# Post-norm gains reduced inside the merge, block sums of h formed ahead of attention, and four more chunks as block products

## The chip, the cores and the metric

The kernel runs on one core of a Trainium2 chip. The metric is device time in microseconds, as the median of runs of the whole kernel; a profiled execution gives the trace. Engines are called by their names in the profile: PE is TensorE (matmuls; PEld its weight loads), DVE is VectorE, ACT is ScalarE, POOL is GpSimd, SP is the engine whose queue issues nearly all transfers.

## The reference

One layer of a backbone works on x (512 tokens x 1024) with 256 context tokens, all in fp32:

```python
sh, sc, gt = _modulation(c, w_mod, b_mod)          # silu(c) @ w_mod + b_mod, three parts of 1024
h = _rmsnorm(x, pre_g) * (1.0 + sc) + sh           # hc likewise, from ctx and c_ctx
parts = _split_in(h @ w_in)                        # 10 parts of 1024 columns
b_gate, c_gate, x_in, z_a, q, k, v, z_b, g_a, g_b = parts
attn = _neighbourhood_attention(rope(q), rope(k), v, k_c, v_c, rpb)   # 16 heads of 64
y_a = (silu(z_a) * b_gate * _dwconv3(c_gate * x_in, conv_w, conv_b)) @ w_out_conv
y_b = (silu(z_b) * attn) @ w_out_attn
merged = sigmoid(g_a) * y_a + sigmoid(g_b) * y_b
x = x + gt * _rmsnorm(merged @ w_o, post_g)
```

The part `gt` of the modulation, times `post_g`, scales each channel of the normed output. The kernel calls these products the gains.

## The kernel before, in words

**Precision.** Every fp32 operand of a large product is held as two terms, H (a cast of the value on ACT, L67) and L (the value less H, on DVE, L70). A product is three matmuls: H·H, H·L, L·H. The helper is `split`.

**Chunks.** Weights come as chunks of 256 columns x 1024 rows, two raw tiles of 512 KB each (L89), three raw buffers per half. A chunk is used in one of two ways. Directly, it is split (two 1024-column casts and subtractions) and gives two units of 128 columns: each is 8 x 3 matmuls with 512 tokens moving (L164 to L166). Or it becomes a *pair* (`pair`, L294, with `product`, L286): the 2 x 2 blocks of weights and of h (256 tokens x 512 rows) are multiplied in seven block products in place of eight, 12 matmuls of 256 columns for each, 84 in all (L289). For that the weights' sums T1 to T4 are formed on DVE (L102 to L110), seven blocks are split in two, and results are put together by copies on ACT and adds on DVE (L306 to L317). It also needs four block sums of h, named S2, S3, S4 and X1; `block_sums` forms them once for each of four slices k. `paired` decides which chunk is a pair.

**Stages.** A first stage computes the modulation from slabs of w_mod (a multiply and reduce of 128 x 1024 on DVE for each, L379), normalises x, and multiplies h by a first set of conv columns while h comes into being. Then follow conv chunks for j=1 to 3 with the modulation of the context (`modulate_c`) between their units. The gains, eight more slabs and reductions (`gain`, L571), follow in the same stage. Behind it come queries, keys and values of the first heads (to about 137 us).

Attention walks 8 head pairs p=0 to 7 (to about 500 us), each in eight slots. PE would idle between a slot's scores and its softmax, so `plan` gives each p other chunks as filling: "qk" queries and keys of the next p, "v" values, "zb" the gate of attention's values, "cx" and "bz" conv chunks, "g" merge gates. The block sums stand in slots of p=0 and p=1. The last gate of attention's values, `gate2(3)`, comes behind the last slot.

The merge, j=0 to 7 (534 to 662 us), multiplies conv results `us` and attention results `as` by output chunks y0 to y7 (`in_wout`), with 24 + 24 matmuls each, between the remaining merge gates. At j=4 the scaled gains are copied to a 128 x 128 tile for each k (L977) and transposed by PE (L978) into `gpost`, which lies along the channels. From j=4 on, the last product is prepared: the blocks of w_o are loaded (L925), their sums T1 to T4 formed (L929), and splits made. The last product (L1008) is also in seven blocks; post norm, gains and the residual follow.

**What sets the order.** The first stage is scheduled by hand. For the rest a scheduler orders each engine's instructions by its own estimate; each engine then runs its list strictly in that order. The SP queue also is one list: a transfer that waits for a free buffer holds the later ones. The tiles' tags say which memory a tile shares: `h0` to `h7` hold h, `hc` its context counterpart, `u`, `a` and `s` tags have changing contents.

Of the kernel before, what the change touches and what calls it, by code (L numbers as in the profile page):

```python
# [27 lines left out]
def layer(ctx: ExitStack, tc, xp, ctxt, ctxT, cc, wmod, small, wfirst, win, wout, wo, rel, tab, out):  # L28
# [30 lines left out]
    hcs = [thc[k // 2][:, k % 2] for k in range(KT)]  # L59
    hc = [t[:, 0] for t in hcs], [t[:, 1] for t in hcs]  # L60
    usc = [dr.tile([P, S], F32, name=f"usc{j}") for j in range(KT)]
    asc = [dr.tile([P, 2, S], F32, name=f"asc{g}") for g in range(2)]

    def split(H, L, src, scale=None, pinned=False):

        if scale is None:
            cast = nc.scalar.copy(H, src)  # L67
            if pinned:
                tc.keep_in_program_order(cast)
            nc.vector.tensor_sub(L, src, H.bitcast(F32))  # L70
# [160 lines left out]
        "cx": lambda j: win[2 * j], "bz": lambda j: win[2 * j + 1],  # L231
    }
    def paired(n, i):
        return n == "g" or n == "qk" and i in (3, 4, 6) or n == "zb" and i < 3 or n in ("cx", "bz") and i > 4

    order = [(win[i], False) for i in range(8)] + [(qk(0), False), (vz(0, 0), False)]
    order += [(where[n](i), n if paired(n, i) else False) for f in plan for n, i in f] + [(vz(3, 1), paired("zb", 3))]
# [109 lines left out]
    def unit(w, i, m=hx):  # L347
        ps = pj()
        proj_T(ps, w, i, m)
        return ps  # L350


    with ExitStack() as p0:
# [78 lines left out]
        with tc.manual_schedule(engines={E.PE, E.DVE, E.Activation, E.SP}):  # L432
# [74 lines left out]
            for k in range(KT):  # L507
# [51 lines left out]
        def modulate_c(k):  # L559
            if k < 5:  # L560
                load_slab(k)
            condition(k, 1)
            nc.scalar.mul(cols[k, 1][:, 0:1], cols[k, 1][:, 0:1], sp[:, PG + k:PG + k + 1])
            modulate(k, 1, ctT[k], hc[0][k], hc[1][k])

        def gain(k):

            t = st.tile([P, D], F32, name="wm", bufs=6)
            nc.sync.dma_start(t, wmod[16 + k])
            junk = st.tile([P, D], F32, name="junk")  # L570
            nc.vector.tensor_tensor_reduce(  # L571
                out=junk, in0=t, in1=cb[:, 0], scale=1.0, scalar=sp[:, BM + 16 + k:BM + 17 + k],
                op0=ALU.mult, op1=ALU.add, accum_out=gains[:, k:k + 1],
            )

        ks = [5, 6, 7, 0, 1, 2, 3, 4]
        work = [lambda k=k: modulate_c(k) for k in ks] + [lambda k=k: gain(k) for k in range(KT)]
        for j in range(2, 4):
            for _ in conv(j):
                for f in work[:2]:  # L580
                    f()
                del work[:2]
        for f in work:
            f()
        nc.vector.tensor_mul(gains, gains, sp[:, QG:QG + KT])


    def block_sums():

        h0, h1 = slice(0, 256), slice(256, S)  # L590
        for n in ("S2", "S3", "S4", "X1"):
            blocks_h[n] = [], []
        for k in range(4):
            a, b = (cv.tile([P, S], F32, name="tc", bufs=3) for _ in range(2))
            for x, i in ((a, k), (b, 4 + k)):
                nc.vector.tensor_add(x, hx[0][i].bitcast(F32), hx[1][i].bitcast(F32))
            nc.vector.tensor_sub(b[:, h1], b[:, h1], a[:, h1])
            nc.vector.tensor_sub(a[:, h1], a[:, h0], a[:, h1])
            for o, x, y in ((a[:, h0], b[:, h1], a[:, h0]), (b[:, h0], a[:, h0], b[:, h0])):
                nc.vector.scalar_tensor_tensor(out=o, in0=x, scalar=-1.0, in1=y, op0=ALU.mult, op1=ALU.subtract)  # L600
            yield
            for x, names, tag in ((a, ("S2", "S3"), f"u{k}"), (b, ("S4", "X1"), ("a2", "a3", "s0", "s1")[k])):
                t = hp.tile([P, 2, S], F32R, name=f"{names[0]}{k}", tag=tag)
                split(t[:, 0], t[:, 1], x)
                for n, ts in zip(names, (h0, h1)):
                    for y in range(2):
                        blocks_h[n][y].append(t[:, y, ts])
            yield
# [218 lines left out]

    for g in (keys_queries(0), values(0)):
        for _ in g:
            pass  # L830
    later.pop()[0]()
    convs = {j: conv_pairs(j) if paired("cx", j) else conv(j) for j in range(4, KT)}
    fill = []
# [115 lines left out]
    for j in range(KT):  # L949
        w = chunk()  # L950
        g = [G[j][:, i] for i in range(2)]
        if j in (4, 6):
            raws[j // 2] = G[j]
        m2 = raws[j // 2][:, j % 2]
        for i in range(2):
            nc.vector.scalar_tensor_tensor(
                out=g[i], in0=g[i], scalar=1.0, in1=unit(w, i, ua[i]), op0=ALU.add, op1=ALU.mult
            )
            if j == 7 and i == 0:
                A2 = [bp.tile([P, 2, S], F32R, name=f"A2{k}", tag=f"us{k}") for k in range(4)]  # L960
                for k in range(3):
                    split(A2[k][:, 0], A2[k][:, 1], raws[2 + k // 2][:, k % 2])
        nc.vector.tensor_add(m2, g[0], g[1])
        if j < 4:
            for _ in merge_gates(j + 4):
                pass
        if j == 4:

            nc.vector.tensor_scalar(out=gains[:, 0:4], in0=gains[:, 0:4], scalar1=0.5, scalar2=None, op0=ALU.mult)
            nc.vector.tensor_scalar(out=gains[:, 4:8], in0=gains[:, 4:8], scalar1=-0.5, scalar2=None, op0=ALU.mult)  # L970
            gpost = bp.tile([P, D], F32, name="gpost")
            for i in range(2):
                gb = cv.tile([P, S], F32, name="ta")
                ps = pj()
                for k in range(4):
                    n = 4 * i + k
                    nc.vector.tensor_copy(gb[:, k * P:(k + 1) * P], gains[:, n:n + 1].broadcast_to([P, P]))  # L977
                    nc.tensor.transpose(ps[:, k * P:(k + 1) * P], gb[:, k * P:(k + 1) * P], ident)  # L978
                nc.scalar.copy(gpost[:, i * S:(i + 1) * S], ps)
        if j == 4:  # L980
            A11, S3 = operand("A11", hp, ("u2", "u3")), operand("S3", hp, ("a2", "a3"))
            for q in range(2):
                split(A11[q][:, 0], A11[q][:, 1], raws[q][:, :, h0])
                x = cv.tile([P, S], F32, name="tb").rearrange("p (k c) -> p k c", k=2)
                nc.vector.tensor_sub(x, raws[q][:, :, h0], raws[q][:, :, h1])
                split(S3[q][:, 0], S3[q][:, 1], x)
            B11, B12 = quarter("B11", hp, ("s0", "s1")), quarter("B12", hp, ("u0", "u1"))
            B22, B21, T2, T3 = (quarter(n, hp, (f"h{2 * i}", f"h{2 * i + 1}")) for i, n in enumerate(("B22", "B21", "T2", "T3")))
            for t, i in ((B11, (0, 0)), (B12, (0, 1)), (B22, (1, 1)), (B21, (1, 0))):
                load_block(t, *i)  # L990
# [213 lines left out]
```

## Time and profile before

| | |
|---|---|
| median of 3 runs | 708.93 us (708.57 to 709.4) |
| profiled execution | 709.01 us, span 707.2 us |
| granted clock of PE | 0.997 |
| busy PE / DVE / ACT | 695.0 / 586.3 / 436.5 us |
| matmul instructions on PE | 4196 |
| pairs among the chunks | 20 |
| moved from memory | 87.07 MB read, 5.24 MB written |

The rows of the profile name a line, an engine, an operation, the tiles written and read, and a count. The profile's page gives busy times and the chain that ended last, other views give each engine's waits, and the trace can be cut into stretches. The prediction below quotes the rows that it uses.

### The profile page before, as it was taken

How to read it: one execution, taken by the hardware profiler on the slowest of the kernel's cores; microseconds unless marked ns; L12 is line 12 of the kernel's file. 1: busy time of each engine (PE TensorE's matmuls, PEld its weight loads, DVE VectorE, ACT ScalarE, POOL GpSimd, SP SyncE). 2: the span in 40 equal slices, each digit the busy share in tenths (PEclk: the TensorE clock that was granted, in tenths of full speed). 3: DMA queues.
4: the chain of work that ended last, by engine and by line, in shares of the span. 5: the costliest groups of instructions: out<-in, count | busy, mean ns of one | idle time of the engine just before them, and what ended most of it. 6: DMA issues, size and time to landing. Idle time of an engine off the chain costs nothing.

```text
span 707.2 us, 11426 instructions
## 1 busy us (share of the span) xinstructions
PE 695.0 (98%) x4196; PEld 618.0 (87%) x4196; DVE 586.3 (83%) x1114; ACT 436.5 (62%) x868; POOL 66.9 (9%) x110
## 2 busy tenths in 40 slices
PE   7999999999999999999999999999999999999996
PEld 4888888888889989898999999999898899988885
DVE  6979997668599989978898797999799676665996
ACT  6566632656577677775876766778693444442563
POOL 0000002230130310301302203000000000000000
PEclk9999999999999999999999999999999999999998
DMA  8996896564351563542635436313733233560013
GB/s 338 406 354 227 284 339 173 131 164 144 99 105 24 135 176 116 127 138 60 168 106 165 103 125 157 101 61 105 247 117 116 87 120 120 198 250 30 31 59 120
DMA packets 37466, 108.27 MB, mean 153 GB/s; under 512 B 5025, under 2 KB 5281, under 8 KB 37410
## 3 DMA queue, kind: packets, MB, share of 16 engines
q1 hardware_dynamic: 28946, 92.20, 37.8%
q0 software_dynamic: 8320, 15.21, 10.7%
q8 instruction: 33, 0.54, 0.3%
q14 instruction: 23, 0.19, 0.1%
q10 hardware_dynamic: 144, 0.13, 0.1%
HBM read 87.07 MB, written 5.24 MB: 131 GB/s over the span
## 4 chain that ended last, share of the span: by engine, by line
PE 91%; DVE 4%; DMA 2%; ACT 1%; issue 1%; SPq 0%; POOL 0%; DVEq 0%; ACTq 0%
PE ps L289 25%; PE ps L164 11%; PE ps L166 11%; PE ps L165 11%; PE ps L177 6%; PE ps L1008 5%; PE ps L773 4%; PE ps L754 3%; PE ps L182 3%; PE ps L717 3%; PE ps L196 2%; PE ps L424 2%; PE ps L428 2%; PE ps L425 2%; DMA fraw<-in_wfirst 1%; PE ps L726 1%
## 5 line engine op out<-in xcount | busy, mean ns | idle before, releaser
L67 ACT CAST w<-raw 128x512 fp32r<-128x512 f32 (+1 forms) x193 | 137.3, 733 | 95.9 <-PE ps L166 31.3
L70 DVE TENSOR_TENSOR w<-raw,w 128x512 fp32r<-128x512 f32 (+1 forms) x193 | 156.6, 824 | 42.3 <-ACT w L67 40.9
L289 PE MATMUL ps<-S,w 128*128 128x256 f32 x960 | 121.9, 283 | 0.0
L289 PEld LDWEIGHTS ps<-S,w 128*128 128x128 f32 x960 | 118.2, 192 | 0.1
L289 PE MATMUL ps<-h,w 128*128 128x256 f32 x720 | 94.0, 284 | 0.6 <-DVE tc L306 0.5
L289 PEld LDWEIGHTS ps<-h,w 128*128 128x128 f32 x720 | 89.9, 191 | 2.5 <-DVE tc L306 0.7
L164 PE MATMUL ps<-h,w 128*128 128x512 f32 x208 | 81.5, 392 | 0.0
L166 PE MATMUL ps<-h,w 128*128 128x512 f32 x208 | 81.2, 390 | 0.0
L165 PE MATMUL ps<-h,w 128*128 128x512 f32 x208 | 81.0, 390 | 0.0
L626 POOL DMA_DIRECT2D tc<-tb x32 | 28.8, 1175 | 286.7 <-DVE tc L624 197.7
L747 ACT ACTIVATE pt<-pt,z 128x512 f32<-128x512 f32 x64 | 43.0, 724 | 6.0 <-DVE z L745 5.9
L166 PEld LDWEIGHTS ps<-h,w 128*128 128x128 f32 x208 | 39.0, 188 | 8.3
L165 PEld LDWEIGHTS ps<-h,w 128*128 128x128 f32 x208 | 39.1, 188 | 8.0
L164 PEld LDWEIGHTS ps<-h,w 128*128 128x128 f32 x208 | 39.1, 188 | 7.9
L67 ACT CAST TH<-ps 128x512 fp32r<-128x512 f32 x64 | 35.8, 589 | 15.5 <-PE ps L754 15.5
L733 DVE CUSTOM_DVE_ANT_1 ps<-ps,bt 128x512 f32<-128x512 f32 x56 | 38.8, 693 | 6.8 <-PE ps L717 6.5
L70 DVE TENSOR_TENSOR TL<-ps,TH 128x512 fp32r<-128x512 f32 x64 | 42.2, 682 | 1.0 <-ACT TH L67 0.7
L754 PE MATMUL ps<-ident,pt 128*128 128x128 f32 x256 | 33.3, 273 | 0.0
L177 PE MATMUL ps<-w,h 128*128 128x512 f32 x128 | 32.3, 394 | 0.0
L754 PEld LDWEIGHTS ps<-ident,pt 128*128 128x128 f32 x256 | 29.2, 140 | 2.1 <-ACT pt L747 0.2
L740 ACT ACTIVATE pt<-ps,m 128x512 f32<-128x512 f32 x32 | 22.0, 688 | 12.5 <-DVE m L733 11.8
L773 PE MATMUL ps<-TH,V 128*128 128x256 f32 (+1 forms) x96 | 28.5, 319 | 0.2 <-ACT TH L67 0.2
(249 smaller groups left out, 1387.8 us busy)
## 6 DMA issues: line engine op xcount, KB each, us to landing
raw<-in_win SPq DMA_DIRECT2D x74, 512.0 KB, 4.4
wm<-in_wmod SPq DMA_DIRECT2D x34, 512.0 KB, 6.4
raw<-in_wout SPq DMA_DIRECT2D x16, 512.0 KB, 3.6
bt<-in_rel SPq DMA_DIRECT2D x16, 256.0 KB, 2.9
tc<-tb POOLq DMA_DIRECT2D x32, 128.0 KB, 3.6
B<-in_wo SPq DMA_DIRECT2D x8, 512.0 KB, 6.4
fraw<-in_wfirst SPq DMA_DIRECT2D x8, 384.0 KB, 8.6
qd<-qd POOLq DMA_DIRECT2D x24, 128.0 KB, 2.3
```

The lines of the kernel that those rows point to most:

```text
L67: cast = nc.scalar.copy(H, src)
L70: nc.vector.tensor_sub(L, src, H.bitcast(F32))
L164: nc.tensor.matmul(ps, lhsT=H[k][:, cs], rhs=mH[k], start=k == 0, stop=False)
L165: nc.tensor.matmul(ps, lhsT=H[k][:, cs], rhs=mL[k], start=False, stop=False)
L166: nc.tensor.matmul(ps, lhsT=L[k][:, cs], rhs=mH[k], start=False, stop=k == KT - 1)
L177: nc.tensor.matmul(ps, lhsT=mH[k][:, ts], rhs=both[k].rearrange("p a c -> p (a c)"), start=k == 0, stop=False, skip_group_check=True,)
L289: nc.tensor.matmul(ps, lhsT=w[:, x, k], rhs=act[y][k], start=start and k + o == 0, stop=k == 3 and o == 2, skip_group_check=True,)
L733: nc.vector.tensor_tensor_reduce(out=s3, in0=s3, in1=bt[:, e::4 - e][:, 0:2], scale=-1.0, scalar=3.0e38, op0=ALU.add, op1=ALU.min, accum_o ...
L747: nc.scalar.mul(x, x, z[:, i:i + 1])
L754: nc.tensor.transpose(tp[:, c], pt[:, c * P:(c + 1) * P], ident)
L773: nc.tensor.matmul(o3[:, dst], lhsT=V[p][:, kt, h], rhs=src(t), start=n == 0 and t is TH, stop=n == len(work) - 1 and t is TL,)
L1008: nc.tensor.matmul(out, lhsT=a(x, k, ts), rhs=w[y][k // 2][:, k % 2, cols], start=start and k + o == 0, stop=k == 3 and o == 2, skip_group ...
```

## The change

It has three parts.

1. `paired` also takes in qk 2, zb 3, cx 4 and bz 4, which makes 24 pairs.
2. `block_sums` is stepped during the conv chunks j=2 and 3, once the context's modulation has been handed out, and then during the first queries, keys and values; it no longer stands in attention's slots.
3. The gains leave the conv stage. The conditioning vector after its silu is kept in a DRAM tile `csc`. In the merge, at j=4 and j=5, it is loaded again to all partitions (`cond`, in h4's memory), and the eight slabs follow through h5 to h7. Their scaling, copies and transposes move from j=4 to j=6 in the program. The blocks T2 and T3 of the last product, which use h4 to h7, come after them.

```diff
@@ layer
+    csc = dr.tile([1, D], F32, name="csc")
@@ paired
-        return n == "g" or n == "qk" and i in (3, 4, 6) or n == "zb" and i < 3 or n in ("cx", "bz") and i > 4
+        return n == "g" or n == "qk" and i in (2, 3, 4, 6) or n == "zb" or n in ("cx", "bz") and i > 3
@@ first stage
+            nc.sync.dma_start(csc, cb[0:1, 0])
             nc.sync.dma_start(cb[:, 1], cc[1:2].broadcast_to([P, D]))
@@ conv stage
-        def gain(k):
-
-            t = st.tile([P, D], F32, name="wm", bufs=6)
-            nc.sync.dma_start(t, wmod[16 + k])
-            junk = st.tile([P, D], F32, name="junk")
-            nc.vector.tensor_tensor_reduce(
...
-        ks = [5, 6, 7, 0, 1, 2, 3, 4]
-        work = [lambda k=k: modulate_c(k) for k in ks] + [lambda k=k: gain(k) for k in range(KT)]
+        ks = [5, 6, 7, 4, 0, 1, 2, 3]
+        work = [lambda k=k: modulate_c(k) for k in ks]
+        sums = block_sums()
         for j in range(2, 4):
             for _ in conv(j):
                 for f in work[:2]:
                     f()
+                if not work:
+                    next(sums)
                 del work[:2]
-        for f in work:
-            f()
-        nc.vector.tensor_mul(gains, gains, sp[:, QG:QG + KT])
@@ ahead of attention
     for g in (keys_queries(0), values(0)):
         for _ in g:
-            pass
+            next(sums, None)
@@ attention's slots
-    sums = block_sums()
...
-        if i in (4, 5, 6, 7, 12, 13, 14, 15):
-            next(sums)
@@ merge, for j in range(KT)
         if j == 4:
-
+            A11, S3 = operand("A11", hp, ("u2", "u3")), operand("S3", hp, ("a2", "a3"))
...
+            for t, i in ((B11, (0, 0)), (B12, (0, 1)), (B22, (1, 1)), (B21, (1, 0))):
+                load_block(t, *i)
+        if j in (4, 5):
+            if j == 4:
+                cond = hp.tile([P, D], F32, name="cond", tag="h4")
+                nc.sync.dma_start(cond, csc.broadcast_to([P, D]))
+            for k in range(4 * j - 16, 4 * j - 12):
+                t = hp.tile([P, D], F32, name=f"wg{k}", tag=f"h{5 + k % 3}")
+                nc.sync.dma_start(t, wmod[16 + k])
+                nc.vector.tensor_tensor_reduce(
+                    out=t, in0=t, in1=cond, scale=1.0, scalar=sp[:, BM + 16 + k:BM + 17 + k],
+                    op0=ALU.mult, op1=ALU.add, accum_out=gains[:, k:k + 1],
+                )
+        if j == 6:
+
+            nc.vector.tensor_mul(gains, gains, sp[:, QG:QG + KT])
             nc.vector.tensor_scalar(out=gains[:, 0:4], in0=gains[:, 0:4], scalar1=0.5, scalar2=None, op0=ALU.mult)
```

Three places show what the scheduler makes of it. The first is SP's queue in the merge, from the last blocks of w_o (`B`) to the input for the residual (`xr`); `raw<-in_wout` are the halves of y6 and y7. Before:

```order
L925 DMA B_7013<-in_wo 128x1024
L925 DMA B_7017<-in_wo 128x1024
L89 DMA raw<-in_wout 128x1024 x4
L1062 DMA xr_7237<-in_xp 128x1024
L1062 DMA xr_7238<-in_xp 128x1024
```

Now (`wg` are the gains' slabs):

```order
L914 DMA B_7212<-in_wo 128x1024
L970 DMA cond<-csc 128x1024
L973 DMA wg_7227<-in_wmod 128x1024
L973 DMA wg_7230<-in_wmod 128x1024
L973 DMA wg_7233<-in_wmod 128x1024
L90 DMA raw<-in_wout 128x1024
L973 DMA wg_7236<-in_wmod 128x1024
L90 DMA raw<-in_wout 128x1024
L973 DMA wg_7302<-in_wmod 128x1024
L973 DMA wg_7305<-in_wmod 128x1024
L973 DMA wg_7308<-in_wmod 128x1024
L90 DMA raw<-in_wout 128x1024
```

The load of cond and four slabs stand ahead of the second half of y6, four more slabs by y7's second half.

The second is DVE's list behind the first evictions of j=4 in the merge (`g_6233` before, `g_6453` now: one tile of gates times products). Before:

```order
L929 TENSOR_TENSOR T_7020<-B_7012,B_7014 128x1024
L956 SCALAR_TENSOR_TENSOR g_6233<-g_6233,ps 128x512
L929 TENSOR_TENSOR T_7021<-B_7013,B_7015 128x1024
L70 TENSOR_TENSOR w<-raw,w 128x4x256
L956 SCALAR_TENSOR_TENSOR g_6233<-g_6233,ps 128x512
L70 TENSOR_TENSOR w<-raw,w 128x4x256
L963 TENSOR_TENSOR g_6233<-g_6233 128x512
L956 SCALAR_TENSOR_TENSOR g_6419<-g_6419,ps 128x512
```

Now, where `L974 ISA wg` is a gain's reduction and `ISA gains` the read of its sum:

```order
L945 SCALAR_TENSOR_TENSOR g_6453<-g_6453,ps 128x512 x2
L974 ISA wg_7227,gains<-wg_7227,cond,sp 128x1024
L974 ISA gains 128x1
L952 TENSOR_TENSOR g_6453<-g_6453 128x512
L974 ISA wg_7230,gains<-wg_7230,cond,sp 128x1024
L974 ISA gains 128x1
L974 ISA wg_7233,gains<-wg_7233,cond,sp 128x1024
L974 ISA gains 128x1
L945 SCALAR_TENSOR_TENSOR g_6639<-g_6639,ps 128x512
L71 TENSOR_TENSOR w<-raw,w 128x4x256
```

The reductions stand between the evictions and the splits of y6, and the two sums into T (L929) are no longer there.

The third is PE's list around the gains' transposes (`ps<-ident,ta`). Before they stand at the end of j=4:

```order
L165 MATMUL ps<-as_6157,w 128x512
L166 MATMUL ps<-as_6157,w 128x512
L978 MATMUL ps<-ident,ta 128x128 x8
L164 MATMUL ps<-us_5956,w 128x512
L165 MATMUL ps<-us_5956,w 128x512
```

Now they stand within the first unit of j=7:

```order
L165 MATMUL ps<-us_6176,w 128x512
L166 MATMUL ps<-us_6176,w 128x512
L167 MATMUL ps<-us_6176,w 128x512
L165 MATMUL ps<-us_6179,w 128x512
L166 MATMUL ps<-us_6179,w 128x512
L990 MATMUL ps<-ident,ta 128x128
L167 MATMUL ps<-us_6179,w 128x512
L165 MATMUL ps<-us_6182,w 128x512
L166 MATMUL ps<-us_6182,w 128x512
L990 MATMUL ps<-ident,ta 128x128 x7
L167 MATMUL ps<-us_6182,w 128x512
```

One transpose comes after five matmuls of the unit, the other seven after three more.

More of the change, by code (lines that the diff above doesn't have):

```diff
@@ L350, in unit, with block_sums @@
         return ps
+    def block_sums():
+        h0, h1 = slice(0, 256), slice(256, S)
+        for n in ("S2", "S3", "S4", "X1"):
+            blocks_h[n] = [], []
+        for k in range(4):
+            a, b = (cv.tile([P, S], F32, name="tc", bufs=3) for _ in range(2))
+            for x, i in ((a, k), (b, 4 + k)):
+                nc.vector.tensor_add(x, hx[0][i].bitcast(F32), hx[1][i].bitcast(F32))
+            nc.vector.tensor_sub(b[:, h1], b[:, h1], a[:, h1])
+            nc.vector.tensor_sub(a[:, h1], a[:, h0], a[:, h1])
+            for o, x, y in ((a[:, h0], b[:, h1], a[:, h0]), (b[:, h0], a[:, h0], b[:, h0])):
+                nc.vector.scalar_tensor_tensor(out=o, in0=x, scalar=-1.0, in1=y, op0=ALU.mult, op1=ALU.subtract)
+            yield
+            for x, names, tag in ((a, ("S2", "S3"), f"u{k}"), (b, ("S4", "X1"), ("a2", "a3", "s0", "s1")[k])):
+                t = hp.tile([P, 2, S], F32R, name=f"{names[0]}{k}", tag=tag)
+                split(t[:, 0], t[:, 1], x)
+                for n, ts in zip(names, (h0, h1)):
+                    for y in range(2):
+                        blocks_h[n][y].append(t[:, y, ts])
+            yield
     with ExitStack() as p0:
@@ L564, in modulate_c @@
             modulate(k, 1, ctT[k], hc[0][k], hc[1][k])
-        def gain(k):
-            t = st.tile([P, D], F32, name="wm", bufs=6)
-            nc.sync.dma_start(t, wmod[16 + k])
-            junk = st.tile([P, D], F32, name="junk")
[L571 to L574, printed above, removed]
-        ks = [5, 6, 7, 0, 1, 2, 3, 4]
-        work = [lambda k=k: modulate_c(k) for k in ks] + [lambda k=k: gain(k) for k in range(KT)]
+        ks = [5, 6, 7, 4, 0, 1, 2, 3]
+        work = [lambda k=k: modulate_c(k) for k in ks]
+        sums = block_sums()
         for j in range(2, 4):
@@ L581, in layer @@
                     f()
+                if not work:
+                    next(sums)
                 del work[:2]
-        for f in work:
-            f()
-        nc.vector.tensor_mul(gains, gains, sp[:, QG:QG + KT])
[L588 to L608, printed above, removed]
     attn = {}
@@ L967, in layer @@
         if j == 4:
+            A11, S3 = operand("A11", hp, ("u2", "u3")), operand("S3", hp, ("a2", "a3"))
+            for q in range(2):
+                split(A11[q][:, 0], A11[q][:, 1], raws[q][:, :, h0])
+                x = cv.tile([P, S], F32, name="tb").rearrange("p (k c) -> p k c", k=2)
+                nc.vector.tensor_sub(x, raws[q][:, :, h0], raws[q][:, :, h1])
+                split(S3[q][:, 0], S3[q][:, 1], x)
+            B11, B12 = quarter("B11", hp, ("s0", "s1")), quarter("B12", hp, ("u0", "u1"))
+            B22, B21, T2, T3 = (quarter(n, hp, (f"h{2 * i}", f"h{2 * i + 1}")) for i, n in enumerate(("B22", "B21", "T2", "T3")))
+            for t, i in ((B11, (0, 0)), (B12, (0, 1)), (B22, (1, 1)), (B21, (1, 0))):
[13 more added lines that the diff above has]
+            nc.vector.tensor_mul(gains, gains, sp[:, QG:QG + KT])
             nc.vector.tensor_scalar(out=gains[:, 0:4], in0=gains[:, 0:4], scalar1=0.5, scalar2=None, op0=ALU.mult)
@@ L979, in layer @@
                 nc.scalar.copy(gpost[:, i * S:(i + 1) * S], ps)
[L980 to L990, printed above, removed]
         if j == 5:
```

## The prediction

> **What bounds the kernel now.** I read the page's busy times and the shares of its chain first, then TensorE's waits, then stretches of the trace by engine.
>
> ```profile
> PE 695.0 (98%) x4196; PEld 618.0 (87%) x4196; DVE 586.3 (83%) x1114; ACT 436.5 (62%) x868; POOL 66.9 (9%) x110
> PE 91%; DVE 4%; DMA 2%; ACT 1%; issue 1%; SPq 0%; POOL 0%; DVEq 0%; ACTq 0%
> PE ps L472 <- ACT crow L444: 3.3, 1, 3.3
> PE ps L424 <- ACT h L67: 1.2, 1, 1.2
> PE ps L289 <- DVE tc L306: 0.5, 1, 0.5
> PE ps L773 <- DVE TL L70: 0.5, 1, 0.5
> ```
>
> TensorE is 98% busy and makes 91% of the chain. It waits some 6 us in all, 4.5 of them before its first long stretch. So the time is the sum of the matmuls, and a change counts by the matmul time it removes, less the waits it creates. Behind it VectorE is busy 83%, which is little room, and unevenly spread. From here "late" means later against TensorE than before.
>
> **What a chunk gains as a pair.** A chunk of 256 output columns is either two units of 24 matmuls, each 512 columns wide, or a pair of 84 matmuls, each 256 wide. Both stand side by side in the gates and merges behind attention (chain of waits: start, length, work):
>
> ```profile
> 514.24 20.15 PE ps L289 x168
> ...
> 545.30 10.07 PE ps L289 x84
> 555.37 0.23 PE ps L164
> ...
> 566.28 10.07 PE ps L289 x84
> ```
>
> A pair takes 10.07 us (168 take 20.15: the same). Between 555.37 and 566.28 stand two units: 10.91 us for 48 matmuls, 0.227 each against 0.120. The pair saves 0.84 us. The order of the changed kernel holds 2016 matmuls of L289's kind where 1680 stood, four pairs more, so the edit is really there. **Term 1: 4 x 0.84 = 3.36 us less.**
>
> [...]
>
> **What it asks of VectorE and ScalarE.** Groups by shape (busy, mean ns | idle before):
>
> ```profile
> L70 DVE TENSOR_TENSOR w<-raw,w 128x512 fp32r<-128x512 f32 x143 | 95.7, 685 | 17.0 <-ACT w L67 15.7 <-PE ps L754 0.8
> L70 DVE TENSOR_TENSOR w<-raw,w 128x1024 fp32r<-128x1024 f32 x50 | 60.9, 1221 | 25.3 <-ACT w L67 25.2
> L102 DVE TENSOR_TENSOR raw<-raw 128x512 f32<-128x512 f32 x20 | 13.7, 685 | 0.2
> L306 DVE TENSOR_TENSOR tc<-tc,ps 128x256 f32<-128x256 f32 x12 | 4.9, 412 | 0.0
> L314 DVE SCALAR_TENSOR_TENSOR tc<-tc 128x256 f32<-128x256 f32 x12 | 5.0, 420 | 1.1 <-ACT tc L311 1.1
> L571 DVE CUSTOM_DVE_ANT_0 junk<-wm,cb,sp 128x1024 f32<-128x1024 f32 x8 | 10.3, 1282 | 0.0
> ```
>
> A pair needs 4 weight sums and 7 splits of 0.685 us and 4 evictions of about 0.415: 9.2 us. Two splits of 1.221 go. So each new pair costs VectorE 6.8 us. Block sums of one k are 4 operations of 512 columns and 4 of 256, 4.4 us; all four k, 17.6 us. The eight gains are about 10.3 us plus reads. Now the stretches that win or lose such work (busy of PE, PEld, DVE, ACT, POOL; clock; DMA share; GB/s):
>
> ```profile
> 40.00:60.00 20.00, 20.00 (x90) 16.32 (x89) 16.35 (x27) 15.10 (x25) 0.00 (x0) 1.00 0.66 235
> 138.00:182.00 44.00, 44.00 (x222) 37.23 (x221) 33.32 (x69) 27.77 (x54) 8.27 (x13) 1.00 0.47 130
> 182.00:224.00 42.00, 42.00 (x244) 36.79 (x243) 35.96 (x86) 28.63 (x68) 8.34 (x13) 1.00 0.37 87
> 486.00:545.00 59.00, 59.00 (x399) 54.51 (x399) 53.76 (x102) 41.78 (x76) 0.00 (x0) 1.00 0.44 143
> 545.00:618.00 73.00, 73.00 (x481) 67.28 (x480) 46.27 (x70) 30.64 (x51) 0.00 (x0) 1.00 0.39 131
> ```
>
> *In front of attention.* The gains' 10.3 us go, the 17.6 come. The new order starts the sums early: about 5.6 us of them fall in 40 to 60, where VectorE has 3.65 free, so the weight splits behind them come some 2 us late. Such a split is due about 3 us after it is done. I take 0 (0 to 0.8).
>
> *p=0, 138 to 182.* 10.7 us are free; two pairs add 13.6 and two k of sums leave, 8.8: 4.8 more, covered. What can still stall is a chunk that holds its raw buffers longer, so that the next chunk lands late and ScalarE queues behind its cast: 0 (0 to 0.8).
>
> *p=1, 182 to 224.* A pair adds 6.8, sums take 8.8 away: 2 us of relief, just ahead of three of TensorE's few waits, the last two on VectorE:
>
> ```profile
> 252.55 0.49 PE L773 MATMUL ps<-TH,V 128*128 128x512 f32 x1 [0.16 <-ACT TH L67]
> 253.50 0.50 PE L773 MATMUL ps<-TL,V 128*128 128x512 f32 x1 [0.45 <-DVE TL L70]
> ...
> 263.44 1.69 PE L289 MATMUL ps<-h,w 128*128 128x256 f32 x12 [0.47 <-DVE tc L306]
> ```
>
> They are 1.08 us. The work of p=2 that causes them is unchanged, and it starts behind a sync of TensorE, so I leave them: 0 (1.1 less to 0).
>
> *The last gate, 486 to 545.* 5.2 us free, 6.8 added: up to 1.5 us late until 545, behind which 26.7 are free. Successive VectorE operations overlap a little, so the true excess is nearer the low end. **Term 2: 0.2 us more (0 to 1.5).**
>
> **The gains in the merge.** SP's queue takes the load of cond and nine slabs' worth in all, 0.52 MB each; four stand ahead of output chunk y6's first load, one more ahead of its second. Before:
>
> ```profile
> 615.82 3.91 SPq L925 DMA_DIRECT2D B<-in_wo  x5
> 619.84 11.83 SPq L89 DMA_DIRECT2D raw<-in_wout  x4
> 620.00:624.00 4.00, 4.00 (x19) 3.34 (x18) 3.63 (x6) 3.97 (x6) 0.00 (x0) 1.00 0.91 306
> 624.00:628.00 4.00, 4.00 (x20) 3.30 (x19) 2.51 (x3) 0.08 (x1) 0.00 (x0) 1.00 1.01 383
> 629.01 1.05 ACT L67 CAST w<-raw 128x1024 fp32r<-128x1024 f32 x1 [4.92 <-DMA raw<-in_wout]
> 640.84 0.39 PE L164 MATMUL ps<-us,w 128*128 128x512 f32 x1
> ```
>
> The queue is full (share 1.01, 383 GB/s) until y6 lands at 629.0, and TensorE asks for y6 at 640.84. Four loads at 383 GB/s are 5.5 us: cast at 634.5, split by 636.7, 4 us in hand. The remaining slabs wait for a buffer whose reduction is done, so the eighth reduction ends at about 644 to 647. The scaled gains are copied only behind the eviction of j=6, after 651.7, so 4 us are in hand there too. Behind each reduction VectorE queues the splits of y6 and y7 and the merge's evictions. This costs 0 as long as the queue keeps its rate.
>
> *The transposes.* Eight move from the end of j=4 into j=7's first unit:
>
> ```profile
> 629.06 1.04 PE L978 MATMUL ps<-ident,ta 128*128 128x128 f32 x8
> 662.60 11.04 PE L1008 MATMUL ps<-w,A 128*128 128x512 f32 x48
> 651.72 0.39 PE L164 MATMUL ps<-us,w 128*128 128x512 f32 x1
> 626.53 1.23 DVE L929 TENSOR_TENSOR T<-B,B 128x1024 f32<-128x1024 f32 x1 [1.25 <-DMA B<-in_wo]
> 656.16 2.36 DVE L929 TENSOR_TENSOR T<-B,B 128x1024 f32<-128x1024 f32 x2
> L977 DVE COPY ta<-gains x8: 218/222/223, 538.6 to 543.2; 128x128 f32<-128x128 f32 x8
> 663.71 1.22 DVE L70 TENSOR_TENSOR w<-B,w 128x1024 fp32r<-128x1024 f32 x1
> 665.44 1.22 DVE L70 TENSOR_TENSOR w<-B,w 128x1024 fp32r<-128x1024 f32 x1
> 666.58 0.69 DVE L70 TENSOR_TENSOR A<-g,A 128x512 fp32r<-128x512 f32 x1
> ```
>
> Their own time is the same in both places. But before, the copies were long done; now each follows j=6's eviction (0.7), a scale and its copy. The first transpose stands 1.1 us into the unit, the other seven 1.9 us in, while the copies, at 0.22 each, end some 3.2 us in. TensorE waits there, and behind it the rest of that unit. **Term 3: 0.4 us more (0.2 to 1.0).**
>
> *The tail.* Two sums of the output weights, 1.2 us each, that ran by 628 (the second at 626.53), and the eight copies now stand between 652 and 665 on VectorE, together 4 us, with only a short gap to swallow them: the sums end about 3 us late. Behind them are the splits at 663.71 to 666.58. TensorE needs these from 668.05 (24 of the 48 matmuls from 662.60) to about 670, so they had 2.7 to 3.4 us in hand. **Term 4: 0.4 us more (0 to 1.0).**
>
> **Sum.** -3.36 + 0.2 + 0.4 + 0.4 = -2.36 us. The profiled execution took 709.01 (span 707.2), 0.08 over the median: 706.65 there, **706.6** as a median.
>
> **Rivals.**
> (A) *VectorE takes the bound's place.* Terms 2 to 4 at their ends (1.5, 1.0, 1.0), or p=0 for one of them: 3.4 of 3.36 eaten, about 708.9. For it: the last gate's stretch is overbooked, and the tail's margins match its delay. Against: 26.7 us free right behind the gate.
> (B) *The merge's loads come late,* which is the slower case. The nine loads are 4.72 MB, 12.3 us at 383 GB/s. At half that they take 24.6; less the 4 us in hand and 1 more that the tail can give, the last gain, the copies and the sums behind them stall the output by some 7 us: -3.36 + 7 gives 712.6. It decides from about 5 us of lateness, a rate under some 270 GB/s. For it: single stretches of 4 us run lower when buffers block SP. Against: 306 and 383 in the rows above.
> (C) *More than the matmuls:* the 1.08 us of waits around 252 to 263 go too, and terms 2 and 4 stay at 0: 705.3.
> (D) *Narrow matmuls are bound by weight loads* where these pairs stand. The break-even is 10.91/84 = 0.130 us; at a load's own busy time of about 0.19 a pair would take 16 us and the kernel some 20 us more, near 729.
>
> ```profile
> L289 PEld LDWEIGHTS ps<-S,w 128*128 128x128 f32 x960 | 118.2, 192 | 0.1
> ```
>
> The pairs quoted hold 0.120 with the same loads, so this gets next to nothing. [...]
>
> **How the numbers follow.** Forecast 0.64, A 0.18, B 0.08, C 0.09, D 0.01. The forecast's own range is 705.3 to 707.8, from its terms' bounds. With A inside and half of C, leaving out B, D and C's far half, the range is 705.0 to 709.4. About 0.2%, 1.4 us, is what a measurement can tell: faster means below 707.5. The forecast less its upper edge plus C give 0.71; A and that edge 0.19; B, D and the worst of A 0.10.
>
> **What would show it.** In the changed profile: pairs of 10.07 us for the chunks of p=0, p=1 and the last gate; no new TensorE wait ahead of 500; ScalarE's cast of y6 about 5 us later against TensorE, but ahead of j=6; a short wait of the transposes on the copies in j=7; a wait under 1 us in the output's second product on VectorE. A wait of j=6 or of the transposes on a DMA would be B; several waits after 486 that name VectorE, A. The prediction is wrong if pairs take longer than 10.1 us, or if the waits' sum grows by over 2.5 us.

## The result, and the profile after

The change made the kernel slower: a median of 712.91 us (710.89 to 713.72, 6 runs) against 708.78 for the kernel before (6 runs); ratio 1.005, 95% interval 1.0039 to 1.0062. The profiled execution took 712.79 us with a span of 711.0. The forecast was 706.6 us, in a range of 705.0 to 709.4: the time lies outside it, and moved the other way.

The page of the changed kernel (busy times and chain), and TensorE's waits:

```profile
PE 695.3 (98%) x4340; PEld 623.5 (88%) x4340; DVE 607.8 (85%) x1167; ACT 448.5 (63%) x904; POOL 66.9 (9%) x110
...
PE 72%; DVE 11%; DMA 9%; ACT 4%; issue 3%; POOL 0%; SPq 0%; DVEq 0%; ACTq 0%; POOLq 0%
...
PE ps L746 <- ACT pt L739: 1.2, 1, 1.2
PE ps L990 <- DVE ta L989: 0.8, 1, 0.8
PE ps L290 <- ACT tc L306: 0.8, 1, 0.8
PE ps L290 <- DVE g L307: 0.7, 1, 0.7
PE ps L709 <- ACT pt L736: 0.6, 1, 0.6
PE ps L290 <- ACT tc L301: 0.3, 1, 0.3
```

TensorE was 91% of the chain; now it is 72%, and transfers, VectorE and ScalarE have the rest. The busy time is what it was (695.3 against 695.0), though the work is 3.4 us less by pitch: part of it ran slower, 1.7 us of it by the half clock (a granted clock of 0.50) described below. The list names 4.4 us of new waits.

To see where the time went, I took the start of the same matmul in both traces (the first product of the softmax with the values of each half of a head pair, then the units of the merge, then the output). After less before, in us:

| mark in the trace before | what lies just before it | change | block sums and gains moved, 20 pairs (e2) | block sums moved, cx 4 and bz 4 pairs (c3) |
|---|---|---|---|---|
| 188 | p=0: cx 4, bz 4 | -1.06 | 0.00 | -1.38 |
| 207 | p=1, first half: qk 2 | +1.99 | 0.00 | -1.38 |
| 276 | end of p=1, p=2 | +0.76 | -0.89 | -3.39 |
| 350 | p=4 | +1.84 | -0.88 | -3.38 |
| 486 | end of attention | +1.87 | -0.87 | -3.38 |
| 555 | last gate, merge gates g2 and g3 | +2.70 | -1.08 | -3.32 |
| 652 | merge to j=6, transposes not yet made | +1.79 | -1.98 | -3.33 |
| 663 | j=7 with the transposes | +3.84 | +0.28 | -3.33 |

The changed kernel loses in four places: 3.05 us at p=1, 1.1 us at p=4, 0.8 us around the last gate, and 2.05 us in j=7, of which 0.87 is the transposes' own time, moved there from j=4. The tail behind 663 adds nothing. The two other columns belong to experiments below. Each column is a single profiled run; those of the change and of e2 lie within 0.3 us of their medians, while c3's is the fastest of its five runs.

**p=1.** ScalarE's list there (weight casts that waited for a transfer), then TensorE's two waits, then stretches of 2 to 3 us (busy of PE, PEld, DVE, ACT, POOL; clock; DMA share; GB/s):

```profile
192.20 1.05 ACT L68 CAST w<-raw 128x1024 fp32r<-128x1024 f32 x1 [1.72 <-DMA raw<-in_win]
...
195.52 0.62 ACT L68 CAST w<-raw 128x512 fp32r<-128x512 f32 x1 [1.33 <-DMA raw<-in_win]
196.73 0.62 ACT L68 CAST w<-raw 128x512 fp32r<-128x512 f32 x1 [0.59 <-DMA raw<-in_win]
...
198.23 0.69 ACT L736 ACTIVATE pt<-ps,m 128x512 f32<-128x512 f32 x1
...
188.93 2.55 SPq L90 DMA_DIRECT2D raw<-in_win  x3
194.54 0.33 SPq L90 DMA_DIRECT2D raw<-in_win  x1
```

```profile
199.06 0.50 PE L709 MATMUL ps<-ks,qd 128*128 128x512 f32 x1 [0.61 <-ACT pt L736]
201.43 1.73 PE L746 MATMUL ps<-ident,pt 128*128 128x128 f32 x8 [1.19 <-ACT pt L739]
...
199.00:202.00 3.00, 1.75 (x8) 1.09 (x8) 3.00 (x7) 1.60 (x4) 1.76 (x3) 0.98 0.35 109
202.00:205.00 3.00, 3.00 (x10) 2.56 (x10) 2.92 (x8) 2.69 (x7) 1.81 (x3) 0.50 0.89 149
```

The pair of qk 2 gives its raw buffers back only when its second half is split. So SP issues the loads of the next chunks, v 1 and qk 3, from 188.93 to 194.54, and ScalarE stands still 3.6 us in all for them, with the softmax's exponentials (L736) behind the casts in its list. TensorE's first wait ends on these exponentials.

The second wait has another last link. The exponentials are scaled (L739) by a reciprocal z, and on VectorE z stands behind the four rotary operations of qk 2 (L615, L616):

```profile
198.05 1.29 DVE L615 TENSOR_TENSOR tb<-tc,cosin 128x512 f32<-128x512 f32 x2
199.26 1.29 DVE L616 TENSOR_TENSOR tc<-tc,cosin 128x512 f32<-128x512 f32 x2
200.46 0.16 DVE L737 RECIPROCAL z<-z 128x2 f32<-128x2 f32 x1
200.66 1.34 ACT L739 ACTIVATE pt<-pt,z 128x512 f32<-128x512 f32 x2 [1.39 <-DVE z L737]
```

The sums that z needs were read out on ScalarE by 199.0, so these operations held it for some 1.4 us. The same 1.39 us on z and a second wait of 1.18 us stand in the traces of e3, e8 and c4 below, which keep the pair of qk 2. After both waits TensorE's granted clock is 0.50 from 202 to 205, which costs some 1.7 us more than the waits (an estimate, half of the 3.4 us given at the end): the eight transposes at 201.43 and the six products behind them take 4.00 us, where the same ones take some 2.24 in the trace before (eight transposes 0.79, and six of eight products that take 1.93).

In the trace before there is no weight cast between 186 and 200 at all: v 1 was already split, and the first cast of qk 3 stood at 200.56. The rotary operations of qk 2 came two at a time, at 188 and at 196 (ScalarE, then VectorE):

```profile
181.32 1.04 ACT L67 CAST w<-raw 128x1024 fp32r<-128x1024 f32 x1
200.56 0.62 ACT L67 CAST w<-raw 128x512 fp32r<-128x512 f32 x1
...
188.08 0.69 DVE L623 TENSOR_TENSOR tb<-ps,cosin 128x512 f32<-128x512 f32 x1 [1.30 <-PE ps L166]
195.86 0.69 DVE L623 TENSOR_TENSOR tb<-ps,cosin 128x512 f32<-128x512 f32 x1 [0.99 <-PE ps L166]
```

**j=7.** VectorE's list ahead of the transposes:

```profile
653.48 1.22 DVE L71 TENSOR_TENSOR w<-B,w 128x1024 fp32r<-128x1024 f32 x1
654.61 0.16 DVE L981 TENSOR_SCALAR gains<-gains 128x4 f32<-128x4 f32 x1
654.68 0.68 DVE L945 SCALAR_TENSOR_TENSOR g<-g,ps 128x512 f32<-128x512 f32 x1
655.28 0.16 DVE L982 TENSOR_SCALAR gains<-gains 128x4 f32<-128x4 f32 x1
655.35 0.22 DVE L989 COPY ta<-gains 128x128 f32<-128x128 f32 x1
655.49 0.68 DVE L952 TENSOR_TENSOR g<-g 128x512 f32<-128x512 f32 x1
656.09 1.03 DVE L989 COPY ta<-gains 128x128 f32<-128x128 f32 x7
...
655.62 0.33 PE L990 MATMUL ps<-ident,ta 128*128 128x128 f32 x1 [0.81 <-DVE ta L989]
```

Unit j=6 ended at 653.51, but a split of B stood ahead of its eviction, which therefore began at 654.68. The copies follow, and TensorE waits 0.81 us, plus shorter gaps within the seven (1.01 us for these, where all eight took 1.04 before).

**What held.** A pair in the merge still takes 10.07 us (547.84 to 557.91), and the loads were in time:

```profile
547.84 3.04 PE L290 MATMUL ps<-h,w 128*128 128x256 f32 x24
557.91 0.40 PE L165 MATMUL ps<-us,w 128*128 128x512 f32 x1
636.48 1.05 ACT L68 CAST w<-raw 128x1024 fp32r<-128x1024 f32 x1 [9.64 <-DMA raw<-in_wout]
642.63 0.39 PE L165 MATMUL ps<-us,w 128*128 128x512 f32 x1
649.86 1.28 DVE L974 CUSTOM_DVE_ANT_0 wg<-wg,cond,sp 128x1024 f32<-128x1024 f32 x1
```

y6 was cast 6 us ahead of its use, and the last gain was reduced by 651.15, 2.4 us ahead of the end of j=6.

### The profile page after: what moved, and what is told of

Its sections match the earlier page's. It is cut to its first block, busy times and chain, and to the rows that moved or that the text cites. A ratio compares the mean times of both kernels' runs of the same rounds, so it can differ in the third digit from the quotient of the medians.

```text
span 711.0 us, 11801 instructions
## 1 busy us (share of the span) xinstructions
PE 695.3 (98%) x4340; PEld 623.5 (88%) x4340; DVE 607.8 (85%) x1167; ACT 448.5 (63%) x904; POOL 66.9 (9%) x110
## 4 chain that ended last, share of the span: by engine, by line
PE 72%; DVE 11%; DMA 9%; ACT 4%; issue 3%; POOL 0%; SPq 0%; DVEq 0%; ACTq 0%; POOLq 0%
PE ps L290 21%; PE ps L167 8%; PE ps L166 8%; PE ps L165 8%; PE ps L178 5%; PE ps L1009 5%; DMA raw<-in_win 4%; DVE w L71 3%; PE ps L183 3%; PE ps L746 2%; PE ps L765 2%; PE ps L709 2%; DMA tc<-tb 2%; PE ps L448 2%; PE ps L452 2%
## 5 line engine op out<-in xcount | busy, mean ns | idle before, releaser
L68 ACT CAST w<-raw 128x512 fp32r<-128x512 f32 (+1 forms) x214 | 145.9, 705 | 96.3 <-PE ps L167 23.8
L71 DVE TENSOR_TENSOR w<-raw,w 128x512 fp32r<-128x512 f32 (+1 forms) x214 | 165.7, 789 | 37.6 <-ACT w L68 36.4
L290 PE MATMUL ps<-S,w 128*128 128x256 f32 x1152 | 146.9, 283 | 1.2 <-ACT tc L306 0.8
L290 PEld LDWEIGHTS ps<-S,w 128*128 128x128 f32 x1152 | 141.8, 192 | 2.2 <-ACT tc L306 1.0
L290 PE MATMUL ps<-h,w 128*128 128x256 f32 x864 | 112.9, 284 | 0.7 <-DVE g L307 0.7
L290 PEld LDWEIGHTS ps<-h,w 128*128 128x128 f32 x864 | 107.7, 191 | 3.0 <-DVE g L307 0.9
L165 PE MATMUL ps<-h,w 128*128 128x512 f32 x144 | 56.3, 391 | 0.0
L167 PE MATMUL ps<-h,w 128*128 128x512 f32 x144 | 56.3, 391 | 0.0
L166 PE MATMUL ps<-h,w 128*128 128x512 f32 x144 | 56.1, 389 | 0.0
L739 ACT ACTIVATE pt<-pt,z 128x512 f32<-128x512 f32 x64 | 42.9, 721 | 8.3 <-DVE z L737 8.1
L165 PEld LDWEIGHTS ps<-h,w 128*128 128x128 f32 x144 | 27.0, 188 | 5.6
L166 PEld LDWEIGHTS ps<-h,w 128*128 128x128 f32 x144 | 27.0, 188 | 5.6
L167 PEld LDWEIGHTS ps<-h,w 128*128 128x128 f32 x144 | 27.0, 188 | 5.6
```

What stands on the lines that cost most here:

```text
L165: nc.tensor.matmul(ps, lhsT=H[k][:, cs], rhs=mH[k], start=k == 0, stop=False)
L166: nc.tensor.matmul(ps, lhsT=H[k][:, cs], rhs=mL[k], start=False, stop=False)
L167: nc.tensor.matmul(ps, lhsT=L[k][:, cs], rhs=mH[k], start=False, stop=k == KT - 1)
L290: nc.tensor.matmul(ps, lhsT=w[:, x, k], rhs=act[y][k], start=start and k + o == 0, stop=k == 3 and o == 2, skip_group_check=True,)
L739: nc.scalar.mul(x, x, z[:, i:i + 1])
```

## The experiments

Theory T says that the early pairs lose their gain in p=1, since held raw buffers make loads late for ScalarE's ordered list; the transposes lose about 1 us by their place, and the last gate loses its pair's gain. The rivals: the moves disturb the order (R), VectorE simply has too much work in p=0 and p=1 (V), or the merge's loads are the loss. All ratios are against runs of the kernel before on the same chip.

**e1: the three early chunks direct again**

```diff
-        return n == "g" or n == "qk" and i in (2, 3, 4, 6) or n == "zb" or n in ("cx", "bz") and i > 3
+        return n == "g" or n == "qk" and i in (3, 4, 6) or n == "zb" or n in ("cx", "bz") and i > 4
```

> The change, but with cx 4, bz 4 and qk 2 used directly again; the last gate's pair and both moves stay. Theory T (the loss of p=0 to p=2 comes from the three early pairs, whose longer-held raw buffers make ScalarE wait on transfers with the softmax behind them): by the ledger of the two traces p=0 to p=2 ended 0.76 us late with the pairs, so without them that part returns to 0 or below; the wait at 348 us may stay. Time 710.5 to 712, no matmul clock of 0.5 near 200 us. Rival R (the moved block sums and gains disturb the order in front of and inside attention): the waits near 200 us stay and the time is 713 or more, since 2.5 us of matmul time come back.

Measured: 710.12 us, ratio 1.0013 (1.0004 to 1.0023). 2.5 us of matmul work came back and the kernel became 2.6 us faster than the change. The time is 0.4 us under T's range. No wait and no half clock is left near 200 us; elsewhere there is one, of 3.4 us, behind a wait of 1.20 us at 253.71 (granted clock 0.94 from 253 to 256, 0.50 to 258, 0.74 to 260, and 0.995 over the run, as in the change's trace with its one; the trace is of the slowest of ten runs). R is out as the main cause.

**e2: both moves, pairs as before**

```diff
-        ... n == "qk" and i in (2, 3, 4, 6) or n == "zb" or n in ("cx", "bz") and i > 3
+        ... n == "qk" and i in (3, 4, 6) or n == "zb" and i < 3 or n in ("cx", "bz") and i > 4
```

> Both moves (block sums ahead of attention, gains in the merge) with the pairs of before, 20 in all. Theory T: only the transposes' waits in j=7 (1.1 us) are left, less some relief in p=1: 709 to 710. Rival R (the moves alone cost most of it): 711.5 or more.

Measured: 709.54 us, 1.0007 (0.9995 to 1.0018). As T expects: the moves alone cost little. Its column in the table shows a relief of 0.9 us in p=2 and 2.26 us lost in j=7 (with the 0.87 that had been saved at j=4).

**e3: the gains back in the conv stage and at j=4**

```diff
-        work = [lambda k=k: modulate_c(k) for k in ks]
+        work = [lambda k=k: modulate_c(k) for k in ks] + [lambda k=k: gain(k) for k in range(KT)]
...
-                if not work:
+                if len(work) <= 8:
                     next(sums)
...
-        if j in (4, 5):    # cond, the slabs and reductions in the merge
-        if j == 6:         # scaling, copies, transposes
+        if j == 4:         # scaling, copies, transposes, as before
```

> The change, but with the gains formed in the conv stage and transposed at j=4 as before; pairs and block sums as changed. Theory T: the merge's 1.1 us come back and nothing else does: 711.3 to 712.3. A rival that holds the merge's loads (9 x 0.5 MB) for the cause of the loss expects the whole gain to appear: 706 to 708.

Measured: 710.83 us, 1.0032 (1.0016 to 1.0048), some 1.3 us faster than the change by the two ratios, whose intervals overlap, and still slower than before. The runs spread from 709.3 to 714.9. The merge's loads are not the main loss. The median lies half a microsecond below the expected range; its trace has no half clock (granted 1.00 from 197 to 206) although the waits of p=1 are there (1.07 and 1.18 us).

**e5: the kernel before with the last gate's values as a pair**

```diff
-        return n == "g" or n == "qk" and i in (3, 4, 6) or n == "zb" and i < 3 or ...
+        return n == "g" or n == "qk" and i in (3, 4, 6) or n == "zb" or ...
```

> The kernel before with one edit, the last gate of attention's values as a pair. By the ledger the stretch from 487 to 547 us lost 1.7 us against the 0.84 gained. Theory T (the last gate's pair overfills VectorE there): 709.4 to 710. Rival (the pair gains its 0.84 there and the loss has another cause): 707.9 to 708.2.

Measured: 709.56 us, 1.001 (1.0000 to 1.0019). The pair costs 0.4 us by the medians (0.7 by the ratio) where its matmuls save 0.84. But the profiled execution, the fastest of its runs, is 0.5 us shorter than the trace before, so it does not show what eats the gain.

**e6: qk 2 alone direct again**

```diff
-        return n == "g" or n == "qk" and i in (2, 3, 4, 6) or ...
+        return n == "g" or n == "qk" and i in (3, 4, 6) or ...
```

> The change with qk 2 alone used directly again; cx 4, bz 4 and zb 3 stay pairs. Theory T: it is the row of pairs bz 4, qk 2 that holds the raw buffers until 189 us, so that the loads of v 1 and qk 3 land behind the place where ScalarE's list has their casts. With qk 2 direct its buffers come free as soon as it is split; the waits near 199 and 201 us shrink or go and the clock stays at 1: 709.5 to 711. Rival V (VectorE has too much work in p=0 and p=1 whatever the transfers do): one pair's 6.8 us fewer of some 80 give half of the loss back at most, less the 0.84 us of the pair: 711.5 to 712.5.

Measured: 708.14 us, 0.9986 (0.9973 to 1.0). One pair undone, whose matmuls save 0.84 us, gains 4.5 us (ratios 1.005 and 0.9986); the time is 1.4 us under T's range. SP's queue differs: the last four of these loads, which the change issued from 188.93 to 194.54, go out at 174.4, 176.8, 181.5 and 187.0 (the first of them is the third of the row at 169.22).

```profile
169.22 5.49 SPq L90 DMA_DIRECT2D raw<-in_win  x3
...
176.79 5.08 SPq L90 DMA_DIRECT2D raw<-in_win  x2
...
187.00 0.33 SPq L90 DMA_DIRECT2D raw<-in_win  x1
```

V, by which a part of the loss stays with the other two pairs, is out for those two; but this run takes qk 2's VectorE work, and its place in the list, away along with its late loads.

**e9: the weights of v 1 not loaded**

This is meant to part the two. All instructions on the engines stay, though not all in their order; v 1's casts read the resident rotary tables, so the values of that group and the output are meaningless, and two of 74 loads are left out.

```diff
-        def __init__(self, src):
+        def __init__(self, src, resident=False):
+            if resident:
+                self.raws = [cosin.rearrange("p a (b c) -> p (a b) c", c=256) for _ in range(2)]
+                return
...
-                self.raw[n] = Chunk(self.srcs[n][0])
+                self.raw[n] = Chunk(self.srcs[n][0], n == 14)
```

> The change, but the weights of chunk v 1 are not loaded: its casts and subtractions read the rotary tables that lie in memory since the start, so its result is meaningless while each engine has the same work. It needs no raw buffer, so those of qk 3 load earlier as well. Theory T: ScalarE no longer waits for transfers between 190 and 197 us, the softmax behind is in time, TensorE's waits near 199 and 201 us and the half clock behind them go: 708 to 710. Rival V (VectorE's work is what is too much): 712 to 713.

Measured: 710.3 us, 1.0016 (1.0005 to 1.0027), some 2.4 us faster than the change, a little above T's range. The trace is of the fastest of ten runs (707.33 us), 3 us under the median, so it need not hold for the typical run. In it ScalarE waits for no weights between 186 and 200, one of TensorE's two waits is gone, and so is the half clock (granted 1.00 from 202 to 205, the last row below). A wait of the same product (L712 here, L709 in the change) on the exponentials stays, with another cause:

```profile
194.88 1.29 DVE L618 TENSOR_TENSOR tb<-tc,cosin 128x512 f32<-128x512 f32 x2
196.08 1.29 DVE L619 TENSOR_TENSOR tc<-tc,cosin 128x512 f32<-128x512 f32 x2
197.28 0.69 DVE L728 CUSTOM_DVE_ANT_1 ps<-ps,bt 128x512 f32<-128x512 f32 x1
...
198.07 0.69 ACT L739 ACTIVATE pt<-ps,m 128x512 f32<-128x512 f32 x1 [2.67 <-DVE m L728]
...
198.90 0.50 PE L712 MATMUL ps<-ks,qd 128*128 128x512 f32 x1 [0.69 <-ACT pt L739]
202.00:205.00 3.00, 3.00 (x19) 2.67 (x18) 1.67 (x4) 3.00 (x9) 0.00 (x0) 1.00 0.19 32
```

A pair gives both its halves, queries and keys, at its very end. So all four rotary operations stand together on VectorE: here ahead of the row maxima (L728) that the softmax waits for, in the change behind them and ahead of z. The order of the list moved along with the loads, so e9 does not part the two cleanly. Without v 1's loads 2.4 of the 4.5 us came back; how the loss divides between late loads, VectorE's order and the half clock is not shown. What the traces do show is both in the softmax's path: T and V are each right in part, V by order rather than by quantity.

**e8: transposes ahead of j=6's units**

```diff
     for j in range(KT):
+        if j == 6:    # the block of scaling, copies and transposes, moved up
         w = chunk()
```

> The change with the gains' scaling, copies and transposes written ahead of the units of j=6 in place of behind them. Theory T: they no longer follow j=6's eviction, the wait of 0.8 us in j=7 goes, and nothing else moves: 0.8 to 1.1 us under the change. A rival that holds the gains' loads for late expects the wait to reappear in j=6.

Measured: 711.92 us, 1.0035 (1.0024 to 1.0046): some 1 us faster than the change by the ratios, as T expects, with no wait of the transposes left in its trace; the two intervals overlap a little.

**c1 and c2: e6 and e8 together, then the last gate direct as well**

```diff
 c1: e8, and
-        ... n == "qk" and i in (2, 3, 4, 6) or n == "zb" or ...
+        ... n == "qk" and i in (3, 4, 6) or n == "zb" or ...
 c2: also
+        ... n == "qk" and i in (3, 4, 6) or n == "zb" and i < 3 or ...
```

> Two edits undone or mended together: qk 2 direct, and the gains' copies and transposes ahead of the units of j=6. Theory T (the two losses are separate): the median of the variant with qk 2 direct, 708.1, less the 0.7 to 1.1 us that the early transposes gave: 707.1 to 707.5, which beats the kernel before by 1.5 us or more. If the losses were one (VectorE behind everywhere), no more than 708.

> As c1, with the last gate's values direct again. Theory Z (a pair there overfills VectorE between 487 and 547 us, and gives away its 0.84): as fast as c1 or 0.4 us faster, 706.7 to 707.4. If the pair keeps its gain there: 0.8 us slower than c1.

Measured: c1 707.67 us, 0.9984 (0.9974 to 0.9993); c2 707.29 us, 0.9969 (0.9958 to 0.9981). c1 misses its range by 0.2 us, and by the ratios it is only 0.1 us faster than e6. Its trace, of the slowest of eleven runs, shows that TensorE, now earlier, meets the gains again in j=6:

```profile
646.52 1.28 DVE L988 CUSTOM_DVE_ANT_0 wg<-wg,cond,sp 128x1024 f32<-128x1024 f32 x1
...
650.28 1.18 DVE L950 COPY ta<-gains 128x128 f32<-128x128 f32 x8
650.56 0.33 PE L951 MATMUL ps<-ident,ta 128*128 128x128 f32 x1 [0.97 <-DVE ta L950]
```

c2 is in its range; that the last gate is better direct agrees with e5, though the intervals of c1 and c2 overlap.

**c3: no move of the gains**

c3 has the block sums ahead of attention, cx 4 and bz 4 as pairs, qk 2 and zb 3 direct, and the gains as in e3.

```diff
 e3, and
-        return n == "g" or n == "qk" and i in (2, 3, 4, 6) or n == "zb" or n in ("cx", "bz") and i > 3
+        return n == "g" or n == "qk" and i in (3, 4, 6) or n == "zb" and i < 3 or n in ("cx", "bz") and i > 3
```

> Block sums ahead of attention and cx 4, bz 4 as pairs; qk 2 and zb 3 direct, the gains formed in the conv stage as before. It tells what moving the gains is worth once the transposes are no loss: if the conv stage has room for the gains and the sums (VectorE had some 27 us free from 40 to 137 with the gains' time added), it equals c2 within 0.4 us; if VectorE is late there, it is 1 us or more slower.

Measured: 706.36 us, 0.9964 (0.995 to 0.9977), the fastest of all and 2.5 us below the kernel before. By the ratios it is 0.35 us under c2, within the first expectation. In its trace the list of waits holds only two, at the start:

```profile
PE ps L495 <- ACT crow L467: 3.2, 1, 3.2
PE ps L447 <- ACT h L67: 1.2, 1, 1.2
```

So the conv stage has room for the gains as well as the sums, and moving the gains buys nothing that these runs can tell.

**c4 and c5: what c3 rests on**

```diff
 c4: c3 with qk 2 a pair
+        ... n == "qk" and i in (2, 3, 4, 6) or n == "zb" and i < 3 or n in ("cx", "bz") and i > 3
 c5: c3 with cx 4 and bz 4 direct, the block sums' move alone
+        ... n == "qk" and i in (3, 4, 6) or n == "zb" and i < 3 or n in ("cx", "bz") and i > 4
```

> c3 with one edit, qk 2 a pair as in the change. Theory T (the pair of qk 2 behind that of bz 4 makes the loads late for ScalarE's list, whatever else stands): waits near 199 to 202 us again, and 3 to 5 us slower than c3, so 709.5 to 711. If the cost of qk 2 hung on the gains' move or the last gate: 705.5 to 706.5.

> The kernel before with the block sums moved ahead of attention and nothing else (20 pairs, gains in the conv stage). By the ledgers cx 4 and bz 4 are worth 1.7 us to c3 and the sums' leaving p=1 the rest, 0.9 us: 707.8 to 708.2. If the two pairs themselves took the stalls of p=2 away, it equals the kernel before: 708.9.

Measured: c4 711.02 us, 1.0028 (1.0013 to 1.0044); c5 708.93 us, 0.9999 (0.9991 to 1.0008). The pair of qk 2 costs 4.5 us in c3 too (1.0028 less 0.9964), with the same picture, the low clock included (a mean of 0.57 from 203 to 206):

```profile
197.09 0.62 ACT L67 CAST w<-raw 128x512 fp32r<-128x512 f32 x1 [2.43 <-DMA raw<-in_win]
...
200.64 0.50 PE L719 MATMUL ps<-ks,qd 128*128 128x512 f32 x1 [1.50 <-ACT pt L746]
203.01 1.73 PE L756 MATMUL ps<-ident,pt 128*128 128x128 f32 x8 [1.18 <-ACT pt L749]
203.00:206.00 3.00, 2.99 (x12) 2.51 (x13) 3.00 (x9) 2.69 (x7) 2.49 (x3) 0.57 0.79 131
```

c5 missed its range; its time is that of the other expectation, in which the two pairs themselves take the stalls away. Its trace, of the fastest of eleven runs, lies 1.1 us below the one before, but its median does not differ, so the relief in p=2 that the traces of e2 and c5 show is not seen in the typical time. cx 4 and bz 4 then give c3 some 2.5 us (roughly 1.3 to 3.6 by the two intervals), against the 1.68 of their matmuls; whether there is more, and from where, stays open. No run has qk 2 as a pair with cx 4 and bz 4 direct, so whether its pair costs this alone or only behind theirs is not tested.

## Why the prediction was wrong

- **Term 1, the matmuls:** right. The pitch held (a pair takes 10.07 us before and after), and where cx 4 and bz 4 alone are added the gain is there (c3 against c5, 2.5 us).
- **p=1, "2 us of relief":** this step failed, and with it the direction. It counted VectorE's work over 42 us and found less than before, so no wait was set against the 0.84 us that qk 2's pair gains. The pair costs 4.5 us (e6 against the change, c4 against c3). Half of the mechanism was named, but one pair early and too small: "a chunk that holds its raw buffers longer, so that the next chunk lands late and ScalarE queues behind its cast", at 0 to 0.8 us in p=0. p=0 went well; in p=1 late loads held the exponentials. The other half was not named: a pair delivers queries and keys together, and their four rotary operations then held the reciprocal (1.39 us). In the trace, waits of 0.61 and 1.19 us and a half clock worth 1.7 us make 3.5 us; 3.05 are lost there, since part of qk 2's gain stands against them. Buffers, the order of each list and the moment at which a pair delivers decide there, and a sum of busy time shows none of them.
- **The waits at 252 to 263:** the two waits of the value products are gone in the changed trace; 0.33 us remain at 248. By c5 the typical time does not show a gain from this, so taking 0 for them was no error that can be seen.
- **Term 2, the last gate:** 0.2 us of loss was forecast, inside 0 to 1.5. The pair as a whole loses 0.4 us by e5's median, so the loss is about 1.2: right in kind, and mis-sized. In the change's trace 0.74 us of it is a wait at 522.21 for an eviction of the next gates (L307), which stands on VectorE behind the four operations that apply the last gate's values (L777, L778, 519.33 to 521.74). They too come together because a pair gives both halves at its end.
- **Merge loads:** the forecast of 0 was right, and rival B, the slower case, did not happen, though the kernel did get slower. y6 came 6 us early. The last reduction ended 2.4 us ahead of the end of j=6 where 4 were forecast.
- **Term 3, the transposes:** 0.4 us (0.2 to 1.0) was forecast; the trace shows 1.2 us beyond their own time, and e8 gave 1 us. The estimate let the eviction of j=6 begin at once; a split of 1.2 us stood ahead of it.
- **Term 4, the tail:** 0.4 us was forecast and about 0 measured. That TensorE came to the output later, by the wait in j=7, does not explain it by itself: in the traces of e8 and c2, which have little or none of that wait, the first two products of the output take no more than 0.1 us longer than before either. In these two the copies also come earlier, so which of the two keeps the sums in time is not shown.
- **p=4, 1.1 us:** not in the prediction at all. The same two loads as before, beside Pool's transfers, landed later (a cast waited 3.66 us in place of 1.11):

```profile
347.79 0.62 ACT L68 CAST w<-raw 128x512 fp32r<-128x512 f32 x1 [3.66 <-DMA raw<-in_win]
348.73 3.14 PE L290 MATMUL ps<-S,w 128*128 128x256 f32 x24 [0.81 <-ACT tc L306]
```

  It is absent in the traces of e1, e2 and c3, and e6 and c1 have one like it at 440 us. That it is chance in how the transfers interleave is an argument, not shown; it was not tested.
- **Rival A** (VectorE takes the bound's place) had the result's direction up to about no change. It held in part for the last gate and for the rotary operations, by the order of VectorE's list and not by its amount of work; in the largest piece, qk 2's pair, late transfers stand beside it.
- **Sums and signs:** rival C, by its own terms, gives 704.9 us and not 705.3, and the bounds of terms 2 to 4 give 705.8 to 709.1, not 705.3 to 707.8. Neither would have taken in the measured time. Of the signs of being wrong that the prediction named, the waits came: new ones ahead of 500, and 4.4 us of new ones in all where 1.1 us of old ones went.

## What to carry to other kernels

Work that fills gaps in an ordered list must be priced by what stands behind it: how long it holds the buffers that the next loads need, whether those loads are then in time for the place of their casts, and when it delivers its results. A sum of free engine time over a stretch is not sufficient (by the sum p=1 had 2 us of relief, and 3.05 us were lost). When a change bundles several edits of one kind, take them one by one: here two of four pairs gave 2.5 us, one took 4.5 beside them, one 0.4, and the move of the gains that was to make room was not needed.

## What the runs showed of the hardware

TensorE's granted clock fell to 0.50 for 3.4 us inside a running kernel (means of 0.95 from 201 to 202, 0.50 from 202 to 205, 0.85 from 205 to 206), after two waits of 0.61 and 1.19 us (TensorE busy 1.75 of 3.00 us, from 199 to 202). That added 1.7 us (an estimate, half of the 3.4). c4's trace has the like (waits of 1.50 and 1.18 us, then a mean of 0.57 from 203 to 206); the traces of e3 (1.07 and 1.18) and e8 (0.84 and 1.18) have similar waits at the same place and a granted clock of 1.00 from 197 to 206. So the half clock did not follow such waits each time, and what decides is not shown. It may be part of the wider spread of these variants (710.9 to 713.7 for the change, against 708.3 to 709.4 in the same comparison), but it is not needed for a time of this size: one of the change's runs took 713.03 us at a mean granted clock of 0.999, where 3.4 us at half clock would leave at most 0.998 (an estimate, 1 less 1.7/711).
